# Two-layer second block of a fused kernel: the mixers' GpSimd work goes to VectorE and ScalarE, the rotation is done by small transfers, score products alternate between halves, one norm's squares are added on VectorE

## The chip, the cores and the metric

The kernel runs as one program on one core of one Trainium2 chip. The metric is the device time of an execution in microseconds. The kernel before has a median of 1934.74 us over three executions (1932.25 to 1937.94).

In the profile, PE is TensorE's matmul, PEld its weight load, DVE is VectorE, ACT is ScalarE, POOL is GpSimd and SP the engine that issues the weight loads.

## The reference, cut to what matters

Everything is fp32. A first block (a gated recurrence and a sparse attention, then a mixture of experts) turns x (256 tokens, 1024 wide) into a new x. A second block puts 16 learned tokens in front (272 tokens in all) and runs two layers, each a mixer and a gated feed-forward part. The change touches only the second block's layers:

```python
hn = rms_norm(h, norm_mix_g[l])
proj = hn @ w_in[l]
q, k, v, xr, gate = split(proj)                  # 512 columns each
q = apply_partial_rope(rms_norm(q, q_norm_g[l]), cos, sin)   # 4 heads x 2 halves x 64
k = apply_partial_rope(rms_norm(k, k_norm_g[l]), cos, sin)   # first 16 of 64 rotate
o_attn = diff_attention(q, k, v, lam)            # softmax(half 0) - lam * softmax(half 1)
o_rec = rg_lru_branch(xr, gate, ...)             # conv, two gates, a scan, gelu(gate)
h = h + concat(rms_norm(o_attn), rms_norm(o_rec)) @ w_out[l]
hn = rms_norm(h, norm_ffn_g[l])
g, u = split(hn @ w_gu[l])
h = h + (silu(g) * u) @ w_down[l]
```

The rotation takes, in each half of 64 channels, rows 0 to 7 and 8 to 15: x1 cos - x2 sin and x2 cos + x1 sin; the other 48 rows pass.

## The kernel before, in words

In the second block the activations are held with channels on partitions and tokens along the free side: `hT2` is 8 tiles of 128 channels by 272 tokens. A product `lin_f` (L323) makes 128 output channels: for each of 8 input tiles, three matmuls (the weight's high part by the input's high and low parts, the weight's low part by the input's high part), 24 in all, into one PSUM bank. Each weight piece, 128x1024, has to be split first: ScalarE rounds the high part (L1449), and VectorE (L1452) or, where the item says `eng`, GpSimd (L1454) subtracts for the low part. `run` (L294) issues the split of a piece LEAD = 4 products ahead of its use, and the split pieces have LEAD + 1 buffers. PSUM has 8 banks, taken in turn.

`layer2` (L1627) writes a layer as a list of items: four xr products with the convolution (`conv`), four k products (`qkin(4)` to `qkin(7)`) among which stand the recurrence's gates, four q products (`qkin(0)` to `qkin(3)`) among which stand the five steps of the recurrence's arithmetic (`lru1` to `lru5`, each on whole 128x1088 tiles), then four gate products (G), four value products (V), the attention's heads (`scores`, `mix`, `turn`, `value`), and the output product in two parts (R for the recurrence's half). The feed-forward part follows. A planner of the framework, which simulates the program, fixes the order of the instructions on each engine within this list; every engine then runs its own list in order. `high_priority` moves the small chains of a norm ahead.

The places that the change touches:

- `qkin(i)` (L1767): ScalarE takes the product out of PSUM as z (scaled) and as its square; VectorE writes product x cos into `qk`. `rope` (L1783), one product later, multiplies the squares by `comp` into the bank `prs` (L1787), multiplies z by the 128x128 matrix `rot` on TensorE (L1790), multiplies that by sin back into z (L1791) and adds z to `qk` (L1792). z lies in the tag "vin" with two buffers.
- `qk_norm` (L1794): once all eight squares are in `prs`, a chain of small VectorE instructions (L1800 to L1804, among them L209 to L213) makes the norm factors `rq`; `knorm` (L1807) spreads them by TensorE (`ps_rqb`, L1811) and multiplies `qk` by them.
- `lru2` to `lru4`, `gelu1`: four products of two 128x1088 tiles on GpSimd (L1711, L1717, L1718, L1724) and a fifth (L1740).
- G2, G3 and V0 to V3: the low parts of their weights on GpSimd (L1454).
- `rec_r` (L1757): the low part of the recurrence's output on GpSimd.
- `scores(h)` (L1837): for half 0 and then half 1 of a head, two or three products of 64 rows.
- `sum_h` (L1492): the sum of squares over channels for a norm, by TensorE with a column of ones; for each of the 8 tiles three products (two passes each), right after the tile is made. The norm "nm1", ahead of layer 1, has its sums among the down products of layer 0's feed-forward part.

The rest of GpSimd's work in the second block stays: in the feed-forward part, in the splits of the last output products and in the squares of the first norm.

Of the kernel before, what the change touches and what calls it, by code (L numbers as in the profile page):

```python
# [9 lines left out]
F32 = mybir.dt.float32  # L10
# [9 lines left out]
P = 128  # L20
T1 = 256
D = 1024
KT = 8
# [29 lines left out]

CONST = [("cos", T2), ("sin", T2), ("rot", 128)]
KO = {}
# [15 lines left out]
def _shape_constants():  # L71
    k = np.zeros((P, NCONST), np.float32)

    def put(name, a):
        o, w = KO[name]
        k[: a.shape[0], o : o + w] = a

    inv = np.float32(500000.0) ** (-np.arange(0, 16, 2, dtype=np.float32) / np.float32(16))
    ang = np.arange(T2, dtype=np.float32)[:, None] * inv[None, :]
    cos = np.ones((P, T2), np.float32)  # L80
    sin = np.zeros((P, T2), np.float32)
    rot = np.zeros((P, P), np.float32)
    for b in (0, 64):
        cos[b : b + 8] = np.cos(ang).T
        cos[b + 8 : b + 16] = np.cos(ang).T
        sin[b : b + 8] = np.sin(ang).T
        sin[b + 8 : b + 16] = np.sin(ang).T
        for i in range(8):
            rot[b + 8 + i, b + i] = -1.0
            rot[b + i, b + 8 + i] = 1.0  # L90
    put("cos", cos)
    put("sin", sin)
    put("rot", rot)
    return k
# [100 lines left out]
class Kernel:  # L195
# [1295 lines left out]
    def sum_h(self, pool, k, t0, name):  # L1491

        nc = self.nc
        n = T2 - t0
        ch = self.chunks(n)
        if k == 0:
            self.rb = None
            self.pss = self.ps(f"{name}ss")
        for j, (o, _) in enumerate(ch):
            nc.tensor.matmul(self.pss[:, j : j + 1], self.sq[k][:, o : o + P], self.ones[:, 0:1],  # L1500
                             start=(k == 0 and j == 0), stop=(k == KT - 1 and j == len(ch) - 1))
# [28 lines left out]
    def block2(self):  # L1530
        nc = self.nc
        self.rbs = [self.p2.tile([P, T2], F32, name=f"rb{i}", tag="rb") for i in range(4)]
        self.sq, self.pend, self.rb = {}, [], None
        items = []
        for l in range(2):
            items += self.layer2(l)
        yield from self.run(items, self.ph, LEAD, 8, True)
        hT = self.hT2
        for tt in range(2):
            for c in range(2):  # L1540
                ot = self.ph.tile([P, 1024], F32R, name=f"ot{tt}{c}", tag="whi").bitcast(F32)[:, 0:512]
                pt = self.ps(f"ps_out{tt}{c}")
                for k in range(4):
                    nc.tensor.transpose(pt[:, k * P : k * P + P],
                                        hT[:, 4 * c + k, NMETA + tt * P : NMETA + tt * P + P], self.ident)
                nc.scalar.copy(ot, pt)
                nc.sync.dma_start(self.out[tt * P : tt * P + P, c * 512 : c * 512 + 512], ot)

    def consts2(self, p2):
# [8 lines left out]

        self.cosT, self.sinT, self.rot = const("cos"), const("sin"), const("rot")

# [64 lines left out]
    def layer2(self, l):  # L1625
# [19 lines left out]
        def begin():  # L1645
# [59 lines left out]
        def lru2():  # L1705
            th, c, y, t = B["rr"], B["xc"], B["ry"], B["rt"]

            nc.vector.scalar_tensor_tensor(t, th, 1.0, c, op0=ALU.add, op1=ALU.mult)
            nc.vector.scalar_tensor_tensor(c, t, 2.0, c, op0=ALU.subtract, op1=ALU.mult)

            nc.gpsimd.tensor_tensor(t, y, y, op=ALU.mult)  # L1711

        def lru3():
            th, c, y, t, ii = B["rr"], B["xc"], B["ry"], B["rt"], B["ii"]
            nc.vector.scalar_tensor_tensor(t, t, -0.5, th, op0=ALU.mult, op1=ALU.mult)
            nc.vector.scalar_tensor_tensor(y, t, 1.5, y, op0=ALU.add, op1=ALU.mult)
            nc.gpsimd.tensor_tensor(ii, ii, c, op=ALU.mult)  # L1717
            nc.gpsimd.tensor_tensor(y, y, th, op=ALU.mult)  # L1718

        def lru4():  # L1720
            th, c, y, t, ii = B["rr"], B["xc"], B["ry"], B["rt"], B["ii"]

            nc.vector.tensor_scalar(y[:, :, 0:1], th[:, :, 0:1], 0.5, 0.5, op0=ALU.mult, op1=ALU.add)
            nc.gpsimd.tensor_tensor(ii, ii, y, op=ALU.mult)  # L1724
            nc.vector.tensor_scalar(t, c, -2.0, -1.0, op0=ALU.mult, op1=ALU.add)
# [32 lines left out]
        def rec_r():  # L1758
            hr = B["ry"]
            r = self.col_rows(B["recr"], T2, f"rec{l}")  # L1760
            for n in range(4):
                nc.vector.scalar_tensor_tensor(hr[:, n], hr[:, n], self.col("recg", 4 * l + n), r,
                                               op0=ALU.mult, op1=ALU.mult)
                self.split(part("yhi", 4 + n), part("ylo", 4 + n), hr[:, n], nc.gpsimd)


        def qkin(i):  # L1767
            def f(po):
# [8 lines left out]
                nc.scalar.activation(sq, po, AF.Square)  # L1777
                nc.vector.scalar_tensor_tensor(B["qk"][:, i], po, g, self.cosT, op0=ALU.mult, op1=ALU.mult)  # L1778
                if i != 4:
                    rope()  # L1780
                B["qs"] = i, sq, z
            return f

        def rope():
            i, sq, z = B["qs"]
# [50 lines left out]
        def scores(h):  # L1836
            def f():  # L1837
# [4 lines left out]
                mx = tile_(f"mx{h}", [P, 3, 2], tag="mx2", bufs=2)  # L1842
                pss = []
                for c in range(2):
                    s = slice(64 * c, 64 * c + 64)
                    ps = self.ps(f"ps_sc{l}{h}{c}")
                    nc.tensor.matmul(ps[:, 0:T2], qk[s, h, 144:272], qk[s, 4 + h, :], start=True, stop=True)
                    nc.tensor.matmul(ps[:, T2:416], qk[s, h, 16:144], qk[s, 4 + h, 0:144], start=True, stop=True)
                    if l == 0:
                        nc.tensor.matmul(ps[0:16, 416:432], qk[s, h, 0:16], qk[s, 4 + h, 0:16], start=True, stop=True)  # L1850
                    pss.append(ps)
                for c in range(2):
# [190 lines left out]
```

## Time and profile before

| | |
|---|---|
| median of three executions | 1934.74 us (1932.25 to 1937.94) |
| the profiled execution, its own time | 1937.82 us |
| its span, first to last instruction | 1936.1 us |
| busy over the span: PE / DVE / ACT / POOL | 1739.4 / 810.0 / 568.3 / 264.4 us |
| mean granted clock of TensorE | 0.935 of full |

The second block starts at about 1200 us and fills the rest of the span. Its layer 0 mixer lies at 1203 to 1362 us, layer 1's at 1590 to 1728 us. The time of an instruction is that between its start and its end, and instructions of one engine can overlap a little, so that start-to-start differences are the safer measure. The granted clock is 1.00 at 2.4 GHz and 0.50 at 1.2 GHz. A releaser in brackets is what ended the engine's idle time before the row.

### The profile page before, as it was taken

To read this page: it belongs to the slowest core of one execution; us is meant where nothing else is said; L and a number is where in the kernel's file an instruction comes from. 1 tells how busy PE (TensorE), PEld (TensorE's weight loads), DVE (VectorE), ACT (ScalarE), POOL (GpSimd) and SP (SyncE) were. 2 spreads that over 40 slices of the span, in tenths; PEclk is the share of its full clock that TensorE was granted. 3 is DMA by queue.
4 is the path that set the end of the run, shared out by engine and by line. 5 is a ranking of instruction groups with operands and counts; after the bars stand their busy time and mean duration, and the time that the engine had idled before them with its cause. 6 is when DMAs were issued, how large, how long until landed. Compare 5 with 4: busy or idle time off the path is not lost.

```text
span 1936.1 us, 34266 instructions
## 1 busy us (share of the span) xinstructions
PE 1739.4 (90%) x14551; PEld 1231.3 (64%) x14552; DVE 810.0 (42%) x1806; ACT 568.3 (29%) x1127; POOL 264.4 (14%) x259
## 2 busy tenths in 40 slices
PE   6999899866999997799999766989999998889998
PEld 3786743433544543454354334977999998789998
DVE  3573632211122222122222114587666557876653
ACT  2564511100111110011010102525544445354442
POOL 2322300000000000000000001051233103223320
PEclk8999889976999998899999878888999999889999
DMA  9658589999899999999999997220443453125441
GB/s 387 236 183 322 203 351 427 428 428 425 367 428 429 426 426 427 428 425 428 428 426 427 426 428 330 88 88 1 174 174 134 167 206 120 56 95 192 166 152 51
DMA packets 42698, 556.68 MB, mean 288 GB/s; under 512 B 4788, under 2 KB 5964, under 8 KB 8360
## 3 DMA queue, kind: packets, MB, share of 16 engines
q1 hardware_dynamic: 40368, 548.41, 69.4%
q0 software_dynamic: 1200, 4.29, 0.6%
q8 instruction: 116, 1.90, 0.4%
q10 hardware_dynamic: 968, 1.70, 0.3%
q14 instruction: 46, 0.38, 0.1%
HBM read 553.32 MB, written 1.06 MB: 286 GB/s over the span
## 4 chain that ended last, share of the span: by engine, by line
PE 56%; DMA 12%; DVE 5%; ACT 1%; issue 0%; ACTq 0%; POOL 0%; DVEq 0%; POOLq 0%
DMA we<-wexp 12%; PE ps_lin L339 9%; PE ps_lin L340 9%; PE ps_lin L341 9%; PE ps_l L1320 7%; PE ps_u L1320 6%; PE ps_d L1320 6%; PE ps_g L1286 2%; PE ps_c L1383 2%; DVE qk L1792 1%; PE ps_at L1363 1%; PE ps_rqb L1811 0%; PE ps_ri L1686 0%; PE ps_pg L1348 0%; PE nm0ss L1500 0%
## 5 line engine op out<-in xcount | busy, mean ns | idle before, releaser
L339 PE MATMUL ps_lin<-xhi,wh 128*128 128x272 f32 (+1 forms) x1024 | 301.6, 295 | 0.2 <-ACT xhi L1430 0.2
L340 PE MATMUL ps_lin<-xlo,wh 128*128 128x272 f32 (+1 forms) x1024 | 297.3, 291 | 1.0 <-DVE xlo L1431 1.0
L341 PE MATMUL ps_lin<-xhi,wl 128*128 128x272 f32 (+1 forms) x1024 | 297.4, 291 | 0.0
L1320 PE MATMUL ps_d<-we,at 128*32 128x256 f32 (+1 forms) x2048 | 223.0, 482 | 48.5 <-DMA we<-wexp 39.0
L1320 PE MATMUL ps_l<-we,xg 128*32 128x256 f32 (+1 forms) x2048 | 217.2, 461 | 29.7 <-DMA we<-wexp 29.5
L1320 PE MATMUL ps_u<-we,xg 128*32 128x256 f32 (+1 forms) x2048 | 212.4, 454 | 25.5 <-DMA we<-wexp 24.6
L339 PEld LDWEIGHTS ps_lin<-xhi,wh 128*128 128x128 f32 x1024 | 197.4, 193 | 2.8 <-DVE qk L1778 0.8
L340 PEld LDWEIGHTS ps_lin<-xlo,wh 128*128 128x128 f32 x1024 | 197.3, 193 | 1.8 <-DVE xlo L1431 1.4
L341 PEld LDWEIGHTS ps_lin<-xhi,wl 128*128 128x128 f32 x1024 | 197.3, 193 | 0.0
L1320 PEld LDWEIGHTS ps_d<-we,at 128*32 128x32 f32 (+1 forms) x2048 | 90.4, 128 | 165.0 <-issue 102.2
L1320 PEld LDWEIGHTS ps_l<-we,xg 128*32 128x32 f32 (+1 forms) x2048 | 88.6, 123 | 139.4 <-issue 97.2
L1320 PEld LDWEIGHTS ps_u<-we,xg 128*32 128x32 f32 (+1 forms) x2048 | 87.1, 121 | 128.0 <-issue 76.1
L1387 DVE TENSOR_TENSOR hT<-hT,ps_c 128x512 f32<-128x512 f32 x128 | 79.4, 681 | 151.7 <-PE ps_c L1383 151.7
L1406 POOL TENSOR_TENSOR hT<-hT,g 128x1024 f32<-128x1024 f32 x1 | 3.3, 3261 | 946.1 <-DVE ssm L1404 946.1
L1449 ACT CAST wh<-wgu 128x1024 fp32r<-128x1024 f32 x88 | 92.2, 1049 | 122.1 <-PE ps_lin L340 121.4
L1452 DVE TENSOR_TENSOR wl<-wgu,wh 128x1024 fp32r<-128x1024 f32 x88 | 108.2, 1231 | 41.6 <-ACT wh L1449 41.6
L1332 DVE TENSOR_SCALAR gl<-ps_u 128x512 f32<-128x512 f32 (+1 forms) x36 | 20.3, 572 | 217.1 <-PE ps_u L1324 217.1
L1364 ACT COPY at<-ps_at 128x512 f32<-128x512 f32 (+1 forms) x36 | 17.3, 492 | 299.9 <-PE ps_at L1363 299.1
L339 PE MATMUL ps_lin<-ahi,wh 128*128 128x272 f32 (+1 forms) x352 | 100.6, 286 | 0.0
L341 PE MATMUL ps_lin<-ahi,wl 128*128 128x272 f32 (+1 forms) x352 | 100.0, 284 | 0.0
L340 PE MATMUL ps_lin<-alo,wh 128*128 128x272 f32 (+1 forms) x352 | 99.9, 284 | 0.0
L1288 ACT ACTIVATE xg<-ps_g,modc,a2c 128x128 f32<-128x128 f32 (+1 forms) x120 | 43.8, 452 | 171.0 <-PE ps_g L1286 171.0
(677 smaller groups left out, 2920.9 us busy)
## 6 DMA issues: line engine op xcount, KB each, us to landing
we<-wexp SPq DMA_DIRECT2D x192, 2048.0 KB, 27.3
wgu<-wgu SPq DMA_DIRECT2D x22, 2048.0 KB, 7.7
win<-win SPq DMA_DIRECT2D x14, 2048.0 KB, 9.1
wada<-wada SPq DMA_DIRECT2D x12, 2048.0 KB, 7.9
wdn<-wdn SPq DMA_DIRECT2D x16, 1408.0 KB, 6.0
wout<-wout SPq DMA_DIRECT2D x6, 2048.0 KB, 7.7
wint<-wint SPq DMA_DIRECT2D x2, 2048.0 KB, 9.3
wins<-wins SPq DMA_DIRECT2D x1, 1264.0 KB, 28.1
```

Source lines behind the costliest of these rows:

```text
L339: nc.tensor.matmul(po[:m, :nn], hi[:, a], xh[k], start=(k == 0), stop=False)
L340: nc.tensor.matmul(po[:m, :nn], hi[:, a], xl[k], start=False, stop=False)
L341: nc.tensor.matmul(po[:m, :nn], lo[:, a], xh[k], start=False, stop=(k == nk - 1))
L1286: nc.tensor.matmul(p, self.x[:, tt, k * P : k * P + P], oh[:, tt], start=(tt == 0), stop=(tt == 1))
L1288: nc.scalar.activation(xg[:, k], pg[:, (k - k0) * n : (k - k0) * n + n], AF.Identity, scale=self.a2c[:, k : k + 1], bias=self.modc2[:, k : ...
L1320: nc.tensor.matmul(dst[b][s], lhs(k, b), ws[k // 4][:, o : o + wd], start=(k == 0 and b % per == 0), stop=False)
L1332: nc.vector.tensor_scalar(gl[i], pu[i], 7.0, 0.5, op0=ALU.min, op1=ALU.mult)
L1363: nc.tensor.transpose(pt[:, c * P : c * P + P], li[i][:, c * P : c * P + P], self.ident)
L1383: nc.tensor.matmul(pc[s][:, (tt - t0) * wd : (tt - t0) * wd + wd], gt[b][rows[s], tt * P : tt * P + P], y[b // per][rows[s], (b % per) * w ...
L1387: nc.vector.tensor_tensor(a, a, pc[s].rearrange("p (a b) -> p a b", a=per), op=ALU.add)
L1449: nc.scalar.copy(hi, src)
L1452: nc.vector.tensor_tensor(lo, src, hi.bitcast(F32), op=ALU.subtract)
```

## The change

The rotation's matrix product goes. Instead `qkin` issues, on ScalarE's queue, four transfers of 8 partitions by 272 tokens each, which copy rows of z to the other place in a tile `zr` (two of these for the layer, cleared once by GpSimd); the sign moves into the sin table. `rope` multiplies `zr` by sin into a new tile `zs` (tag "vin", the one of z) and adds that to `qk`. The five 128x1088 products of GpSimd go to VectorE, except the square in `lru2`, which goes to ScalarE. The weights' low parts of G2, G3 and V0 to V3 and the low part in `rec_r` go to VectorE. `scores` writes the products of half 0 and half 1 in turn. For "nm1" VectorE adds the squares of tiles 0 to 6 into one tile `nsum`, and TensorE sums only `nsum` and tile 7.

```diff
@@ sum_h
+        few = name == "nm1"
...
+        if few and 0 < k < KT - 1:
+            nc.vector.tensor_tensor(self.nsum[:, :n], (sq[0] if k == 1 else self.nsum)[:, :n], sq[k][:, :n], op=ALU.add)
+        if k == (KT - 1 if few else 0):
             self.pss = self.ps(f"{name}ss")
...
+        for i, a in enumerate(([self.nsum, sq[k]] if k == KT - 1 else []) if few else [sq[k]]):
+            for j, (o, _) in enumerate(ch):
+                nc.tensor.matmul(self.pss[:, j : j + 1], a[:, o : o + P], self.ones[:, 0:1],
...
@@ begin
+            for n in range(2):
+                B["zr", n] = tile_(f"zr{n}", [P, T2])
+                nc.gpsimd.memset(B["zr", n], 0.0)
@@ lru2, lru3, lru4, gelu1
-            nc.gpsimd.tensor_tensor(t, y, y, op=ALU.mult)
+            nc.scalar.activation(t, y, AF.Square)
-            nc.gpsimd.tensor_tensor(ii, ii, c, op=ALU.mult)
-            nc.gpsimd.tensor_tensor(y, y, th, op=ALU.mult)
+            nc.vector.tensor_tensor(ii, ii, c, op=ALU.mult)
+            nc.vector.tensor_tensor(y, y, th, op=ALU.mult)
-            nc.gpsimd.tensor_tensor(ii, ii, y, op=ALU.mult)
+            nc.vector.tensor_tensor(ii, ii, y, op=ALU.mult)
-            nc.gpsimd.tensor_tensor(t, t, gl, op=ALU.mult)
+            nc.vector.tensor_tensor(t, t, gl, op=ALU.mult)
@@ rec_r
-                self.split(part("yhi", 4 + n), part("ylo", 4 + n), hr[:, n], nc.gpsimd)
+                self.split(part("yhi", 4 + n), part("ylo", 4 + n), hr[:, n], nc.vector)
@@ qkin
+                zr = B["zr", i % 2]
+                for o in (0, 8):
+                    for h in (0, 64):
+                        nc.scalar.dma_start(zr[h + 8 - o : h + 16 - o], z[h + o : h + o + 8])
                 if i != 4:
                     rope()
-                B["qs"] = i, sq, z
+                B["qs"] = i, sq, zr
@@ rope
-            prt = self.ps(f"ps_rot{l}{i}")
-            nc.tensor.matmul(prt[:, :T2], self.rot, z, start=True, stop=True)
-            nc.vector.tensor_tensor(z, prt[:, :T2], self.sinT, op=ALU.mult)
-            nc.vector.tensor_tensor(B["qk"][:, i], B["qk"][:, i], z, op=ALU.add)
+            t = tile_(f"zs{i}", [P, T2], tag="vin", bufs=2)
+            nc.vector.tensor_tensor(t, zr, self.sinT, op=ALU.mult)
+            nc.vector.tensor_tensor(B["qk"][:, i], B["qk"][:, i], t, op=ALU.add)
@@ scores
-                    nc.tensor.matmul(ps[:, 0:T2], qk[s, h, 144:272], qk[s, 4 + h, :], start=True, stop=True)
-                    nc.tensor.matmul(ps[:, T2:416], qk[s, h, 16:144], qk[s, 4 + h, 0:144], start=True, stop=True)
...
+                for rows, o, q, w in parts:
+                    for c in range(2):
+                        s = slice(64 * c, 64 * c + 64)
+                        nc.tensor.matmul(pss[c][rows, o : o + w], qk[s, h, q : q + rows.stop], qk[s, 4 + h, 0:w], start=True, stop=True)
@@ the lists
-        G = [inp(1, n, gate(n), pool if n > 1 else None) for n in range(4)]
-        V = [inp(4, n, vin(n), pool) for n in range(4)]
+        G = [inp(1, n, gate(n)) for n in range(4)]
+        V = [inp(4, n, vin(n)) for n in range(4)]
```

## Rows read from the trace of the kernel before

**Rows 1.** Stretches: from:to, length, busy time of engines, TensorE clock, DMA share

```profile
1247.00:1259.00 12.00, 10.72 (x80) 10.04 (x79) 7.32 (x11) 11.72 (x15) 1.39 (x1) 1.00 0.22 93
1254.00:1287.00 33.00, 22.87 (x151) 21.73 (x150) 31.89 (x36) 10.34 (x16) 25.14 (x9) 0.85 0.18 65
1287.00:1296.00 9.00, 9.00 (x55) 7.85 (x53) 3.37 (x7) 1.04 (x1) 0.00 (x0) 0.59 0.00 0
1296.00:1328.00 32.00, 32.00 (x237) 27.44 (x237) 28.19 (x140) 20.64 (x66) 4.87 (x2) 1.00 0.19 67
1500.00:1590.00 90.00, 90.00 (x727) 90.00 (x726) 44.98 (x57) 36.84 (x53) 8.15 (x7) 1.00 0.53 193
```

**Rows 2.** PE's waits from 1240 us on: waiter, releaser, total, times, longest

```profile
PE ps_rqb L1811 <- DVE rq_y L1804: 11.5, 2, 6.1
PE ps_rot L1790 <- ACT z L1775: 10.7, 6, 4.1
PE ps_lin L340 <- POOL ylo L1454: 0.8, 2, 0.5
```

**Rows 3.** PE in order of time: start, length, instruction, idle time before it

```profile
1234.88 0.70 PE L1790 MATMUL ps_rot<-z,rot 128*128 128x272 f32 x2
1235.51 2.05 PE L1686 MATMUL ps_ri<-xc,wrec 64*64 64x272 f32 x16
...
1286.73 2.83 PE L1811 MATMUL ps_rqb<-ident,rq_y 128*64 128x128 f32 x24 [5.42 <-DVE rq_y L1804]
...
1294.88 0.72 PE L1847 MATMUL ps_sc<-qk 64*128 64x272 f32 x2
...
1296.95 0.88 PE L1811 MATMUL ps_rqb<-ident,rq_y 128*64 128x128 f32 x12
...
1557.37 0.72 PE L1500 MATMUL nm1ss<-ones,nm1sq 128*128 128x1 f32 x6
1557.96 0.38 PE L339 MATMUL ps_lin<-ahi,wh 128*128 128x272 f32 x1
...
1664.46 0.74 PE L1847 MATMUL ps_sc<-qk 64*128 64x272 f32 x4
```

**Rows 4.** VectorE's groups, 1210 us to the end: count, busy us, mean ns, idle before

```profile
L1452 DVE TENSOR_TENSOR wl<-win,wh 128x1024 fp32r<-128x1024 f32 x23 | 28.2, 1224 | 21.9 <-ACT wh L1449 21.9
L1792 DVE TENSOR_TENSOR qk<-qk,z 128x272 f32<-128x272 f32 x16 | 19.5, 1219 | 0.2
L1715 DVE SCALAR_TENSOR_TENSOR rt<-rt,rr 128x1088 f32<-128x1088 f32 x2 | 7.2, 3602 | 0.0
L1716 DVE SCALAR_TENSOR_TENSOR ry<-rt,ry 128x1088 f32<-128x1088 f32 x2 | 6.7, 3358 | 0.1
L1725 DVE TENSOR_SCALAR rt<-xc 128x1088 f32<-128x1088 f32 x2 | 5.1, 2556 | 0.0
L1802 DVE TENSOR_SCALAR rqv<-rqv 128x48 f32<-128x48 f32 x2 | 4.3, 2126 | 0.1
L1709 DVE SCALAR_TENSOR_TENSOR xc<-rt,xc 128x1088 f32<-128x1088 f32 x2 | 2.6, 1282 | 0.0
```

**Rows 5.** VectorE in order of time, the addition of a rotation beside an idle GpSimd

```profile
1255.84 0.43 DVE L1792 TENSOR_TENSOR qk<-qk,z 128x272 f32<-128x272 f32 x1
```

**Rows 6.** GpSimd's and ScalarE's groups, same stretch and columns as Rows 4

```profile
L1454 POOL TENSOR_TENSOR wl<-win,wh 128x1024 fp32r<-128x1024 f32 x12 | 33.3, 2785 | 23.4 <-ACT wh L1449 12.0 <-PE ps_sc L1850 11.3
L1449 ACT CAST wh<-win 128x1024 fp32r<-128x1024 f32 x34 | 35.6, 1046 | 86.6 <-PE ps_lin L340 86.6
```

**Rows 7.** ScalarE in order of time, the last q product of layer 0

```profile
1273.24 0.49 ACT L1775 ACTIVATE z<-ps_lin,qgs 128x272 f32<-128x272 f32 x1 [6.75 <-DVE qk L1792]
```

**Rows 8.** Issues on ScalarE's queue: count, ns each (shortest, median, longest), starts

```profile
L824 ACTq DMA_DIRECT2D bt<-bexp x2: 334/346/359, 203.0 to 203.5; - x2
```

**Rows 9.** Transfers by line: queue, count, KB each, median us from issue to landing

```profile
out<-ot SPq DMA_DIRECT2D x4, 256.0 KB, 2.1
bt<-bexp ACTq DMA_DIRECT2D x2, 192.0 KB, 5.5
```

More of the change, by code (lines that the diff above doesn't have):

```diff
@@ L52 @@
 NCOL = _o
-CONST = [("cos", T2), ("sin", T2), ("rot", 128)]
+CONST = [("cos", T2), ("sin", T2)]
 KO = {}
@@ L81, in _shape_constants @@
     sin = np.zeros((P, T2), np.float32)
-    rot = np.zeros((P, P), np.float32)
     for b in (0, 64):
@@ L85, in _shape_constants @@
         cos[b + 8 : b + 16] = np.cos(ang).T
-        sin[b : b + 8] = np.sin(ang).T
+        sin[b : b + 8] = -np.sin(ang).T
         sin[b + 8 : b + 16] = np.sin(ang).T
-        for i in range(8):
-            rot[b + 8 + i, b + i] = -1.0
-            rot[b + i, b + 8 + i] = 1.0
     put("cos", cos)
     put("sin", sin)
-    put("rot", rot)
     return k
@@ L1495, in sum_h @@
         ch = self.chunks(n)
+        sq = self.sq
+        few = name == "nm1"
         if k == 0:
             self.rb = None
+        if few and 0 < k < KT - 1:
+            nc.vector.tensor_tensor(self.nsum[:, :n], (sq[0] if k == 1 else self.nsum)[:, :n], sq[k][:, :n], op=ALU.add)
+        if k == (KT - 1 if few else 0):
             self.pss = self.ps(f"{name}ss")
-        for j, (o, _) in enumerate(ch):
-            nc.tensor.matmul(self.pss[:, j : j + 1], self.sq[k][:, o : o + P], self.ones[:, 0:1],
-                             start=(k == 0 and j == 0), stop=(k == KT - 1 and j == len(ch) - 1))
+        for i, a in enumerate(([self.nsum, sq[k]] if k == KT - 1 else []) if few else [sq[k]]):
+            for j, (o, _) in enumerate(ch):
+                nc.tensor.matmul(self.pss[:, j : j + 1], a[:, o : o + P], self.ones[:, 0:1],
+                                 start=(i == 0 and j == 0 and (few or k == 0)), stop=(k == KT - 1 and a is sq[k] and j == len(ch) - 1))
         if k == KT - 1:
@@ L1532, in block2 @@
         self.rbs = [self.p2.tile([P, T2], F32, name=f"rb{i}", tag="rb") for i in range(4)]
+        self.nsum = self.p2.tile([P, T2], F32, name="nsum")
         self.sq, self.pend, self.rb = {}, [], None
@@ L1557, in const @@
             return t
-        self.cosT, self.sinT, self.rot = const("cos"), const("sin"), const("rot")
+        self.cosT, self.sinT = const("cos"), const("sin")
         self.m2 = m2 = p2.tile([P, 416], F32, name="m2")
@@ L1778, in f @@
                 nc.vector.scalar_tensor_tensor(B["qk"][:, i], po, g, self.cosT, op0=ALU.mult, op1=ALU.mult)
+                zr = B["zr", i % 2]
+                for o in (0, 8):
+                    for h in (0, 64):
+                        nc.scalar.dma_start(zr[h + 8 - o : h + 16 - o], z[h + o : h + o + 8])
                 if i != 4:
                     rope()
-                B["qs"] = i, sq, z
+                B["qs"] = i, sq, zr
             return f
         def rope():
-            i, sq, z = B["qs"]
+            i, sq, zr = B["qs"]
             for j, (o, _) in enumerate(self.chunks(T2)):
@@ L1842, in f @@
                 mx = tile_(f"mx{h}", [P, 3, 2], tag="mx2", bufs=2)
[L1843 to L1846, printed above, removed]
-                    nc.tensor.matmul(ps[:, 0:T2], qk[s, h, 144:272], qk[s, 4 + h, :], start=True, stop=True)
-                    nc.tensor.matmul(ps[:, T2:416], qk[s, h, 16:144], qk[s, 4 + h, 0:144], start=True, stop=True)
-                    if l == 0:
-                        nc.tensor.matmul(ps[0:16, 416:432], qk[s, h, 0:16], qk[s, 4 + h, 0:16], start=True, stop=True)
-                    pss.append(ps)
+                pss = [self.ps(f"ps_sc{l}{h}{c}") for c in range(2)]
+                parts = [(slice(0, P), 0, 144, T2), (slice(0, P), T2, 16, 144)] + ([(slice(0, 16), 416, 0, 16)] if l == 0 else [])
+                for rows, o, q, w in parts:
+                    for c in range(2):
+                        s = slice(64 * c, 64 * c + 64)
+                        nc.tensor.matmul(pss[c][rows, o : o + w], qk[s, h, q : q + rows.stop], qk[s, 4 + h, 0:w], start=True, stop=True)
                 for c in range(2):
```

## The prediction

> **What bounds the kernel now.** I read the page's shares first: TensorE is busy over most of the span, so a change in the second block pays only where TensorE waits, runs at the lower clock, or does work that goes. Then the stretches: in layer 0's feed-forward part TensorE is busy for 90.00 of 90 us at full clock, while from 1254 to 1287 us, where the q products and the recurrence's arithmetic lie, it is busy for 22.87 of 33 us, and VectorE for 31.89 with GpSimd beside it for 25.14 [rows 1]. So that stretch is VectorE's, the feed-forward part TensorE's. Then TensorE's waits: the two largest are the norm factors (11.5 us over the two layers) and z for the rotation (10.7 us) [rows 2]. They are one thing: z of the last q product waits 6.75 us for a buffer that VectorE's addition L1792 holds [rows 7], and the chain for the norm factors stands behind the same VectorE work. TensorE goes on at 1286.73 us [rows 3] and then runs at a mean clock of 0.59 for 9 us [rows 1].
>
> Last, VectorE's groups, for why it is late. The addition L1792 takes 0.43 us with GpSimd idle [rows 5] but 1.219 us in the mean of 16; L1715, L1716 and L1725 take 3.60, 3.36 and 2.56 us where L1709, of the same width and with GpSimd idle, takes 1.28; L1802 takes 2.13 us for 48 columns, less work than the 0.43 us addition of 272 [rows 4, 5]. VectorE stands still beside GpSimd's long instructions. Over both layers this loses 16 x (1.219 - 0.43) = 12.6, 7.2 + 6.7 + 5.1 - 6 x 1.28 = 11.3, and four such halts in the norm-factor chain (two in a layer; L1802's row stands for them) of 2.13 less at most 0.43, some 6.8: in all 30.7 us, 15.4 a layer, nearly all in the 33 us stretch.
>
> **The change part by part**, against the profiled execution's 1937.82 us (span 1936.1 and 1.7 around it), which is 3.1 above the median.
>
> *GpSimd out of the mixers.* VectorE gets back 15.4 us a layer and takes over, before the norm factors, three products of 1088 columns at 1.28 us [rows 4] and five weight pieces at 1.22 us (23 of that shape are there already [rows 4]; GpSimd needs 2.79 us each [rows 6]): 3.8 + 6.1 = 9.9 us. If VectorE stays full up to the norm factors, they come 15.4 - 9.9 = 5.5 us earlier in each layer: the lower end. The upper end is ScalarE. It is busy 11.72 of the 12 us up to 1259 [rows 1]; three projections' transfers at four issues of 0.35 us [rows 8] add 4.2 us and the Square of 1088 columns about 1.05, as the 1024-wide cast [rows 6]: 1264.2 us. Then come two more projections, each a cast of 1.05, a z of 0.49 and a square taken as long [rows 6, 7], with one set of issues (1.4) between: the last square ends at 1269.7 instead of about 1274.2 (1273.24 + 2 x 0.49 [rows 7]), 4.5 us earlier. Behind it the old path took 1286.73 - 1274.2 = 12.5 us, with two halts of the chain (3.4) and the last two additions' halts (about 1.6 together by the mean) in it: 5.0 go. Upper end 9.5 us. I take 7.5: VectorE's full row [rows 1] speaks for the lower end, but the chain is moved ahead of other ready work and needs neither the recurrence's products nor V's weights, which can fall behind it. That is 15 us over two layers. Work that falls behind is paid later: VectorE has 32 - 28.19 us of room up to 1328 us [rows 1].
>
> *The rotation.* One rotation on TensorE costs 0.63 us from start to start (1234.88 to 1235.51) [rows 3]. The two that stand ahead of all the gates delay the recurrence's arithmetic: 1.3 us a layer, 2.5 in all; the other two k rotations, ahead of the table loads and q, move the stretch by up to as much again, and I take 1.5 of it. Rotations of q lie in VectorE's stretch and give nothing. The wait of z on L1792 goes (it is in the term above). What is late next is the transfers: L1792 now waits for four landings. The nearest small transfer lands 2.1 us after its issue, one on ScalarE's queue beside the weight loads 5.5 us [rows 9]. `rope` runs a product later (24 matmuls), which covers the first; behind VectorE's wait stand the next product's x cos and the weight pieces, so a late landing stops TensorE after some products. From 0 to 2.1 us for each of the 8 q projections, 0 to 17; I take 3, since VectorE is behind anyway and the DMA share there is 0.18 [rows 1]. On ScalarE each projection's issues (1.4 us) delay what stands behind them: the next weight cast, which leads by four products, the next z and the gates. For the k products the room is there (the gates lie between), for q it is in the sum above.
>
> The Trainium skill ("DMA: Bandwidth & Descriptors", section "Rules for kernel authors") speaks against this part: transfers under 64 KB are mostly overhead, and many small ones should be joined into a large one. The 64 pieces here are of 8.5 KB. The rows agree that an issue costs the same 0.33 to 0.36 us whatever its size is for [rows 8]; the trace has no transfer this small. By the rule, read as four overheads in series of 2.1 us per projection, the third rival below is what comes.
>
> *Halves in turn.* In layer 0 a head's products take 1296.95 - 1294.88 = 2.07 us, half after half. In layer 1 the planner's order already has both halves' long products side by side: four instructions in 0.74 us where two take 0.72 [rows 3]. So layer 0 gains half of 2.07, 1.03 for each of 4 heads, 4.1 us, and layer 1 nothing. TensorE is full there (32.00 of 32), but VectorE is at 28.19 and gets L1740's product and one more weight piece (2.5 us) for a halt it loses: I take 3, with 0 and 4.1 as ends.
>
> *The norm's squares.* Each of the 8 sums takes 1557.96 - 1557.37 = 0.59 us [rows 3] in the stretch where TensorE is always busy; six go: 3.5 us in full. The six additions are 0.43 us each [rows 5] on a VectorE that is busy 44.98 of 90 us [rows 1]; if that cover failed, 2.6.
>
> *The rest.* `rec_r`'s low part costs TensorE 0.8 us of waits [rows 2]; I take 0.5. The clearing of `zr` lies at a layer's begin beside products; bounds 0 to 1. SP's weight loads wait for pieces to be split, and none of TensorE's larger waits is for them: nothing.
>
> Sum: 15 + 4 - 3 + 3 + 3.5 + 0.5 = 23 us. 1937.8 - 23 = 1914.8 on the profiled execution, which stands 3.1 above the median; so **1912** for the median.
>
> **The rivals.**
>
> *VectorE stays the bound, or waits for landings.* The norm factors come 5.5 us earlier at best, eight landings take some 1.5 each back (12), the scores gain nothing: 11 - 12 + 2.5 + 3.5 = 5 to 10 us, 1925 to 1930. For it: 31.89 of 33. Against it: the DMA share there is low.
>
> *TensorE stops stalling.* With the planner's order now near the truth, the chain comes right behind the last square: 9.5 us a layer, no low clock behind the stall (9 us at 0.59 instead of 1.00, 3.7 us a layer [rows 1]), the full rotation and score terms: 2 x (9.5 + 3.7) + 5 + 4.1 + 3.5 + 0.8 = 40, and 1895. For it: the two waits are 22.2 us [rows 2]. Against it: 9.9 us more work on VectorE.
>
> *The transfers become the pace: slower.* z is freed only by its four landings, and `zs` uses the same two buffers. If that puts cast, z, square, issues and landing in a row, a q projection takes 1.05 + 0.98 + 1.4 + L. The stretch's 151 matmul records in 33 us [rows 1] are about six products of 24, one in 5.5 us, stalls included. With L = 2.1 it is 5.5: the stretch gains nothing. With 5.5, as beside the weight loads, it is 8.9: 3.4 us for each of 8 projections, 27 in all, less 7 of the last three terms: slower by 20, 1955. It decides from L of about 3 on. By the Trainium skill's rule in series (4 x 2.1) it is worse still. Against it: there are two buffers, and the DMA share is 0.18 [rows 1].
>
> *No change.* Gains in the mixers are paid back before the output product, since VectorE's total grows where it had 3.8 us of room; only the 3.5 of the norm and a little stay: 1930 to 1936.
>
> **How the numbers follow.** Forecast (14 to 32 us gained) 0.47; TensorE stops stalling 0.16; VectorE or landings bound 0.18; no change 0.10; slower 0.09. A difference under 0.3% (5.8 us) can't be told from none here. Faster: 0.47 + 0.16 and nearly all of 0.18, so 0.80; same: 0.11; slower: 0.09. The range from 1890 to 1931 holds the first three cases and leaves out most of the last two and the far end of the second.
>
> **What would show it.** Right: L1715, L1716 at about 1.3 us and L1792 at 0.43; TensorE's wait on the norm factors under 4 us a layer; nothing waiting as ps_rot; layer 0's heads at about 1.05 us of score products; 12 instead of 48 nm1ss matmuls. Wrong: TensorE's wait at L1811 as long as before (VectorE bound); VectorE's L1791 or L1792 with idle time released by a DMA of more than 1 us each, or ScalarE's z waiting for landings (third rival); a second half (1296 to 1362) that grew by what the first lost (no change).

## The result: 1915.15 us, and the profile after

The kernel after takes 1915.15 us (median of 4 runs, 1911.26 to 1917.45) against 1934.95 (4 runs): ratio 0.9899, interval 0.9886 to 0.9912. That is 19.8 us less; forecast were 1912 and 22.7. The profiled execution took 1911.26 us, its span 1909.5.

The halts are gone. VectorE's groups (line, operation, tiles, count, busy us, mean ns, idle before) against [rows 4]. The lines have moved: L1715, L1716 and L1725 of the kernel before are L1722, L1723 and L1732 of this one, L1792 is L1802 and L1802 is L1812. The first two take 1.28 us where they took 3.60 and 3.36, the third 0.72 (2.56 before), the additions 0.435 in the mean of 16 (1.219), and the 48 columns 0.18 (2.13).

```profile
L1722 DVE SCALAR_TENSOR_TENSOR rt<-rt,rr 128x1088 f32<-128x1088 f32 x2 | 2.6, 1282 | 0.0
L1723 DVE SCALAR_TENSOR_TENSOR ry<-rt,ry 128x1088 f32<-128x1088 f32 x2 | 2.6, 1281 | 0.0
L1732 DVE TENSOR_SCALAR rt<-xc 128x1088 f32<-128x1088 f32 x2 | 1.4, 716 | 0.0
L1812 DVE TENSOR_SCALAR rqv<-rqv 128x48 f32<-128x48 f32 x2 | 0.4, 184 | 0.0
L1801 DVE TENSOR_TENSOR zs<-zr,sin 128x272 f32<-128x272 f32 x16 | 7.0, 438 | 13.7 <-DMA zr<-z 13.6
L1802 DVE TENSOR_TENSOR qk<-qk,zs 128x272 f32<-128x272 f32 x16 | 6.9, 435 | 0.2
```

But TensorE's wait on the norm factors, 11.5 us in [rows 2], has doubled. From the lists of waits (total, times, longest): TensorE's for the rotation are gone, waits on the squares `qsq` have come, those on the recurrence's low part `ylo` are 1.7 us where they were 0.8 [rows 2], and VectorE waits for the landed rows of `zr`:

```profile
PE ps_rqb L1821 <- DVE rq_y L1814: 22.8, 2, 12.4
PE ps_qs L1798 <- ACT qsq L1784: 6.6, 2, 3.5
PE ps_lin L335 <- DVE ylo L1449: 1.7, 2, 0.9
DVE zs L1801 <- DMA zr<-z: 13.6, 9, 3.3
```

Layer 0 on TensorE (start, us, idle before): the last squares' sums are 3.13 us late, the factors 12.43, and a head's scores take 1.12 us where they took 2.07 [rows 3].

```profile
1264.36 0.84 PE L1798 MATMUL ps_qs<-comp,qsq 128*128 128x16 f32 x6 [3.13 <-ACT qsq L1784]
1277.63 2.83 PE L1821 MATMUL ps_rqb<-ident,rq_y 128*64 128x128 f32 x24 [12.43 <-DVE rq_y L1814]
1284.80 1.12 PE L1859 MATMUL ps_sc<-qk 64*128 64x272 f32 x12
```

VectorE between those two moments: the 13 links of the factors' chain take 0.2 us each, yet it lasts from 1266.42 to 1277.58, because a recurrence product, landings, scans and two weight pieces stand between the links.

```profile
1266.42 0.19 DVE L1810 SCALAR_TENSOR_TENSOR rqv<-ps_qs,r 128x48 f32<-128x48 f32 x1
...
1266.75 1.28 DVE L1731 TENSOR_TENSOR ii<-ii,ry 128x1088 f32<-128x1088 f32 x1
1267.95 0.18 DVE L204 TENSOR_SCALAR rq_y<-rqv 128x48 int32<-128x48 int32 x1
1268.54 0.44 DVE L1801 TENSOR_TENSOR zs<-zr,sin 128x272 f32<-128x272 f32 x1 [0.40 <-DMA zr<-z]
1269.64 0.44 DVE L1801 TENSOR_TENSOR zs<-zr,sin 128x272 f32<-128x272 f32 x1 [0.67 <-DMA zr<-z]
1270.01 1.33 DVE L1736 TENSOR_TENSOR_SCAN ry<-rt,ii 128x272 f32<-128x272 f32 x2
1271.25 0.18 DVE L206 TENSOR_TENSOR rq_t<-rq_y 128x48 f32<-128x48 f32 x1
1271.35 1.33 DVE L1736 TENSOR_TENSOR_SCAN ry<-rt,ii 128x272 f32<-128x272 f32 x2
1272.60 0.77 DVE L1802 TENSOR_TENSOR qk<-qk,zs 128x272 f32<-128x272 f32 x2
...
1275.11 2.35 DVE L1447 TENSOR_TENSOR wl<-win,wh 128x1024 fp32r<-128x1024 f32 x2
1277.38 0.20 DVE L1814 TENSOR_TENSOR rq_y<-rq_y,nm0r_y 128x48 f32<-128x48 f32 x1
```

ScalarE and its queue (ACTq): an issue takes 0.63 us in the median of 64 (least, median and most in ns in the first line), instead of the 0.35 of [rows 8]. In layer 0 the last three issues of a projection take 2.18 us together, and ScalarE's next instruction (ACT_TABLE_LOAD) stands behind them.

```profile
L1789 ACTq DMA_DIRECT2D zr<-z x64: 631/632/1232, 1226.8 to 1626.7; - x64
1242.14 2.18 ACTq L1789 DMA_DIRECT2D zr<-z  x3
1244.36 1.28 ACT L1707 ACT_TABLE_LOAD   x1 [2.12 <-issue]
```

The trace before has one transfer on that queue that is smaller than those of [rows 8], 24 KB at the kernel's start:

```profile
L284 ACTq DMA_DIRECT2D bada<-bada x1: 775/775/775, 1.3 to 1.3; - x1
```

Stretches of the kernel after (busy us of TensorE, weight loads, VectorE, ScalarE, GpSimd; granted clock): q products to factors, factors to scores, and scores. VectorE is busy 24.81 of 28 us in the first, where it was 31.89 of 33 [rows 1]: it now waits, while the clock is 0.79 and then 0.72 of full speed.

```profile
1250.00:1278.00 28.00, 12.44 (x103) 12.24 (x103) 24.81 (x45) 10.82 (x15) 0.00 (x0) 0.79 0.23 80
1278.00:1287.00 9.00, 9.00 (x74) 7.67 (x71) 2.46 (x4) 1.04 (x1) 0.00 (x0) 0.72 0.01 3
1287.00:1319.00 32.00, 27.87 (x214) 24.09 (x213) 27.42 (x140) 20.68 (x65) 0.00 (x0) 0.95 0.19 67
```

The norm's sums are now 12 matmuls (line, instructions, ns):

```profile
L1502 PE MATMUL nm1ss<-ones,nsum x6: 167/250/250, 1570.4 to 1570.9; 128*128 128x1 f32 x6
L1502 PE MATMUL nm1ss<-ones,nm1sq x6: 165/250/250, 1572.1 to 1572.6; 128*128 128x1 f32 x6
```

### The profile page after: what moved, and what is told of

It reads as the page before. It is cut to its first block, busy times and chain, and to the rows that moved or that the text cites. A ratio compares the mean times of both kernels' runs of the same rounds, so it can differ in the third digit from the quotient of the medians.

```text
span 1909.5 us, 34235 instructions
## 1 busy us (share of the span) xinstructions
PE 1698.6 (89%) x14483; PEld 1204.0 (63%) x14484; DVE 798.8 (42%) x1840; ACT 569.4 (30%) x1129; POOL 198.8 (10%) x232
## 5 line engine op out<-in xcount | busy, mean ns | idle before, releaser
L334 PE MATMUL ps_lin<-xhi,wh 128*128 128x272 f32 (+1 forms) x1024 | 297.1, 291 | 0.0
L1315 PE MATMUL ps_d<-we,at 128*32 128x256 f32 (+1 forms) x2048 | 219.6, 475 | 45.9 <-DMA we<-wexp 35.2
L1315 PE MATMUL ps_l<-we,xg 128*32 128x256 f32 (+1 forms) x2048 | 213.2, 452 | 30.0 <-DMA we<-wexp 29.2
L1283 ACT ACTIVATE xg<-ps_g,modc,a2c 128x128 f32<-128x128 f32 (+1 forms) x120 | 43.9, 453 | 170.2 <-PE ps_g L1281 170.2
```

What stands on the lines that cost most here:

```text
L334: nc.tensor.matmul(po[:m, :nn], hi[:, a], xh[k], start=(k == 0), stop=False)
L1283: nc.scalar.activation(xg[:, k], pg[:, (k - k0) * n : (k - k0) * n + n], AF.Identity, scale=self.a2c[:, k : k + 1], bias=self.modc2[:, k : ...
L1315: nc.tensor.matmul(dst[b][s], lhs(k, b), ws[k // 4][:, o : o + wd], start=(k == 0 and b % per == 0), stop=False)
```

## The experiments

Theory: GpSimd's leaving is the gain, and the rest of the change adds little because VectorE and ScalarE, not TensorE, are late at the norm factors. Rivals: the transfers or the alternation carry it; VectorE only moves its work. Ratios are to the kernel before, with 95% intervals; "block" is the second block's length in the profiled execution, from its first product to the output's transposes. Both measures are needed: the work ahead of the second block, whose steps no run changes, takes between 1192.5 us (u_rot) and 1203.3 us (dma_hold) in these traces, so that a time alone does not tell kernels a few us apart.

| kernel | median us | ratio, interval | block us |
|---|---|---|---|
| before | 1934.0 to 1935.0 | 1 | 732.0 |
| after | 1915.15 | 0.9899 [0.9886, 0.9912] | 708.6 |
| u_rot: rotation undone | 1912.80 | 0.9891 [0.9877, 0.9905] | 709.8 |
| u_pool: GpSimd back | 1931.82 | 0.9986 [0.9977, 0.9995] | 724.8 |
| u_sc: alternation undone | 1912.71 | 0.9886 [0.9871, 0.9900] | 708.8 |
| u_nm1: norm's sums undone | 1915.90 | 0.9902 [0.9887, 0.9916] | 711.8 |
| a_pool: GpSimd's leaving alone | 1911.76 | 0.9878 [0.9863, 0.9893] | 716.1 |
| a_pool2: the same again | 1914.75 | 0.9898 [0.9881, 0.9914] | 708.1 |
| rot_sc: GpSimd's leaving, norm's sums | 1909.96 | 0.9876 [0.9859, 0.9892] | 704.4 |
| dma_pool: issued by GpSimd | 1912.05 | 0.9883 [0.9868, 0.9899] | 704.0 |
| hold: recurrence held | 1905.48 | 0.9841 [0.9828, 0.9855] | 701.4 |
| rot_hold | 1906.59 | 0.9849 [0.9835, 0.9862] | 699.0 |
| dma_hold | 1906.57 | 0.9859 [0.9842, 0.9875] | 693.9 |
| rot_sc_hold | 1913.81 | 0.9898 [0.9882, 0.9915] | 708.8 |

Three stages of those traces, each from the start of one TensorE group to the start of the next, layer 0 / layer 1:

| stage (us) | before | after | u_rot | u_pool | a_pool | a_pool2 | dma_pool | hold | rot_hold |
|---|---|---|---|---|---|---|---|---|---|
| gates to norm factors | 51.2 / 51.2 | 48.8 / 47.8 | 45.9 / 45.8 | 52.5 / 51.6 | 45.8 / 45.8 | 45.9 / 45.8 | 45.6 / 45.6 | 43.5 / 44.5 | 40.4 / 40.4 |
| scores to output products | 41.3 / 37.1 | 41.0 / 33.8 | 41.0 / 33.8 | 39.4 / 38.8 | 39.1 / 33.8 | 39.1 / 33.8 | 41.1 / 33.8 | 37.6 / 34.5 | 43.2 / 35.2 |
| from there to `ro*3r` | 19.2 / 18.0 | 17.1 / 15.4 | 20.2 / 15.4 | 21.3 / 19.0 | 19.8 / 18.5 | 15.6 / 17.0 | 17.1 / 17.0 | 20.2 / 17.0 | 18.7 / 14.4 |

**u_rot.** The rotation goes back to TensorE, everything else stays as after.

```diff
...
-                        nc.scalar.dma_start(zr[h + 8 - o : h + 16 - o], z[h + o : h + o + 8])
...
+            nc.tensor.matmul(prt[:, :T2], self.rot, z, start=True, stop=True)
-            nc.vector.tensor_tensor(t, zr, self.sinT, op=ALU.mult)
+            nc.vector.tensor_tensor(z, prt[:, :T2], self.sinT, op=ALU.mult)
...
```

> The changed kernel with the rotation on TensorE again (matrix rot, z rewritten in place, no transfers, no zr). Changed kernel: 1915. Theory: the four issues of a projection take 0.63 us each of ScalarE, 20 us a layer, and hold up the last square, so the transfers give back what the rotation's matmuls cost; without them 1909 to 1917, TensorE's wait for qsq (6.6 us) gone, its wait for the norm factors still 15 us or more, because VectorE's fillers stay. Rival (the rotation by transfers is the larger part of the 20 us gain): 1924 to 1931.

1912.8: the theory's time; the wait on the factors is 7.4 us a layer, 14.8 and just under its "15 or more". The transfers gain nothing; in the stage up to the norm factors they cost 2.9 and 2.0 us. The blocks are as long all the same because two other stretches of layer 0 are shorter with transfers: the first products up to the gates by 3.4 us and the stage behind the first output product by 3.1. In both the clock differs too (0.86 and 0.72 up to `nm0r`, 0.90 and 0.75 behind the output product), so that how much of it is the planner's order no run shows.

**u_pool and a_pool.** GpSimd comes back, or leaves alone (the kernel before with only these lines changed).

```diff
...
-            nc.vector.tensor_tensor(ii, ii, c, op=ALU.mult)
-            nc.vector.tensor_tensor(y, y, th, op=ALU.mult)
+            nc.gpsimd.tensor_tensor(ii, ii, c, op=ALU.mult)
+            nc.gpsimd.tensor_tensor(y, y, th, op=ALU.mult)
...
-        V = [inp(4, n, vin(n)) for n in range(4)]
+        V = [inp(4, n, vin(n), pool) for n in range(4)]
```

> The changed kernel with GpSimd in the mixers again (the five wide products, the low parts of G2, G3, V0 to V3 and of rec_r), the rest as changed. Theory (VectorE's halts beside GpSimd are what the change removes): 1925 to 1934, with L1792's counterpart back at over 1 us and the wide VectorE products at over 3. Rival (moving the work to VectorE only swaps halts for work): 1912 to 1918.

> The kernel before with one of the four parts alone: the second block's mixers without GpSimd (products, sums and splits go to VectorE, the first square of the recurrence to ScalarE). Rotation on TensorE, halves' scores in order and the norm's squares summed tile by tile, as before. Theory (GpSimd's leaving is the gain, and the norm's squares add 3.9 us on their own, as the stage table of the kernel with that part undone shows: 202.4 against 198.5 us): the kernel with the rotation undone was 1912.8, so with 3.9 more 1916.7, forecast 1915 to 1919; the wait of TensorE on the norm factors stays at 6 to 8 us a layer. Rival (the gain needs VectorE to be relieved of the rotation's waits or of scores at once): 1922 to 1930.

The theory's time held for u_pool (1931.82). The additions are back at 1.04 us, the wide instructions L1722, L1723 and L1732 at 2.36, 2.20 and 2.58, not over 3. a_pool went past its theory: 1911.76, all of the gain. Its stretch from the gates to the factors in layer 0 and the same stretch of the kernel before, both with 281 matmuls (columns as above): with GpSimd's 25.14 us gone VectorE is busy 5.3 us less, although it has more to do, and the stretch is 5.4 us shorter. The wait on the factors is 7.4 us a layer. The last line is the recurrence's scans in a_pool's stretch, which came behind the factors before.

```profile
1232.40:1278.20 45.80, 37.15 (x281) 33.64 (x280) 35.81 (x62) 26.13 (x41) 0.00 (x0) 0.96 0.26 93
```

```profile
1235.50:1286.70 51.20, 40.44 (x281) 36.67 (x280) 41.08 (x51) 24.94 (x40) 25.14 (x9) 0.91 0.23 83
```

```profile
L1737 DVE TENSOR_TENSOR_SCAN ry<-rt,ii 128x272 f32<-128x272 f32 x4 | 2.6, 700 | 0.0
```

**a_pool2.** The block of a_pool's trace was 716.1 us long, too long for its median, so the same kernel ran again.

> The kernel with GpSimd's leaving as its only part once more, because its two readings disagree: by the median (1911.76) it has the whole gain, by the second block's length in the trace (716.1 us from its first product to the transposes of the output, 732.0 before, 708.6 after) two thirds. Theory (the length is right, and three of its four runs were fast for a reason that is not the part's: they show a granted clock of 0.949 where the profiled one shows 0.945): most runs 1914 to 1919. Rival (the part alone does give all): most runs 1910 to 1913 again, and this trace's second block is some 708 us long.

It split the two: runs of 1910.81, 1914.7, 1914.8 and 1915.2, and a block of 708.1. The largest difference between the two traces is the clock in one stage. The same 91 matmuls in layer 0's stage behind the first output product (TensorE busy, granted clock), in a_pool and in a_pool2:

```profile
1324.80:1344.70 19.90, 17.03 (x91) 0.74 0.00 1
```

```profile
1327.80:1343.40 15.60, 12.75 (x91) 1.00 0.00 1
```

So the part alone gives 19 to 23 us, and a single trace is good to some 8 us of block length, while its stage up to the norm factors repeats to 0.1.

The same can be read for the whole block. TensorE from the second block's first product to the output's transposes (length, busy us, granted clock) in the kernel before, a_pool, a_pool2 and the kernel after:

```profile
1196.60:1928.60 732.00, 696.90 (x5331) 0.95 0.34 125
1193.40:1909.50 716.10, 688.84 (x5331) 0.96 0.35 128
1197.30:1905.40 708.10, 680.86 (x5331) 0.97 0.35 129
1193.30:1901.90 708.60, 664.74 (x5263) 0.96 0.36 130
```

With GpSimd's leaving alone TensorE's idle time falls from 35.1 to 27.2 or 27.3 us, in both runs alike. The rest, 8.1 us in a_pool and 16.0 in a_pool2, is the same 5331 matmuls taking less time at a higher clock. Up to the norm factors it is VectorE's chain that ends the stage, so those 10.7 us over two layers, alike in both runs, are VectorE's. The other 5.2 us of a_pool and 13.2 of a_pool2 lie in other stages and differ by the clock; what of them GpSimd's leaving causes no run separates. In the kernel after TensorE idles for 43.9 us, more than before; what is saved there is busy time.

**u_sc, u_nm1 and rot_sc.** The halves' scores go back to one half after the other, the norm's squares to 48 matmuls (`few = False`), or rotation and scores both go back.

```diff
-                for rows, o, q, w in parts:
-                    for c in range(2):
+                for c in range(2):
+                    s = slice(64 * c, 64 * c + 64)
+                    nc.tensor.matmul(ps[:, 0:T2], qk[s, h, 144:272], qk[s, 4 + h, :], start=True, stop=True)
...
-        few = name == "nm1"
+        few = False
```

> The changed kernel with the score products half after half again. Theory (in layer 0's head section VectorE is the pace, so TensorE's 4 us there go into waits): 1915 to 1917. Rival (the 4.1 us are saved in full): 1918.5 to 1920.

> The changed kernel with nm1's squares summed by TensorE tile by tile again (48 products). Theory (TensorE is the pace of the feed-forward part): 3.5 us more, 1918 to 1920. Rival (planner's order or waits hide it): 1914 to 1916.

> The kernel after with rotation and scores as before the change: GpSimd out of the mixers and the norm's squares added by VectorE are what is left. Theory (parts add up: 716.1 us for the first alone less 3.9 for the second): length 710 to 713, time 1910 to 1914. Rival (transfers or alternation carry a part of the gain when taken away together): length above 715, time 1916 to 1922.

u_sc came out below both expectations: alternation gives nothing here, and layer 0's stage from scores to output products is 39.1 us without it, 41.0 with it. TensorE in that stage, in the kernel after and in u_sc:

```profile
1284.80:1325.80 41.00, 35.83 (x278) 0.96 0.15 52
```

```profile
1286.90:1326.00 39.10, 38.07 (x277) 1.00 0.15 55
```

With alternation TensorE is idle for 5.2 us, without it for 1.0, and its clock is 0.96 with the waits and 1.00 without. u_nm1's median (1915.9) fits the rival and can't be told from after's, but the stage from `nf0r` to `nm1r` is 202.4 us in it and 198.5 in after. rot_sc, without transfers and alternation, is at 1909.96 no slower than after; its median lies at the lower end of its theory, its block (704.4) below it.

**dma_pool.** The 64 small transfers are issued by GpSimd.

```diff
-                        nc.scalar.dma_start(zr[h + 8 - o : h + 16 - o], z[h + o : h + o + 8])
+                        nc.gpsimd.dma_start(zr[h + 8 - o : h + 16 - o], z[h + o : h + o + 8])
```

> The kernel after with the 64 small transfers of the rotation issued by GpSimd, which has nothing else to do in the mixers, and not by ScalarE. Theory (the issues of 0.63 us each hold ScalarE, and the squares that TensorE waits for come late by it): ScalarE's stalls go, TensorE's waits on the squares (6.6 us between 1180 and 1910) fall under 3, time 1910 to 1913.5, as with the rotation on TensorE. Rival (the landing is the price, or issuing by GpSimd costs more than by ScalarE and halts or delays VectorE): 1915 to 1922, with VectorE's waits for the landed rows above the 13.6 us of the kernel after.

1912.05, within the theory's time, though its interval overlaps that of the kernel after. An issue takes 0.50 us on GpSimd (ns: least, median, most), and VectorE's waits on landings fall from 13.6 to 4.9 us (the last two lines are who waited for the landings, total and times):

```profile
L1789 POOL DMA_DIRECT2D zr<-z x64: 497/499/638, 1230.9 to 1628.5; - x64
...
  ACT z L1782: 7.1, 2
  DVE zs L1801: 4.9, 2
```

The stage up to the factors is 45.6 us in both layers, as short as with the rotation on TensorE: what the transfers cost there goes with their issues when ScalarE is rid of them. The landing is not free: ScalarE's z now waits 7.1 us for it, since its buffer is held until the rows have landed, and TensorE's waits on the squares grew instead of falling (4.8 and 4.6 us in the two layers against 3.1 and 3.5).

**hold.** The recurrence's second half (`lru3` to `lru5`) is held until the factors are done, by a constant that is read from a column written behind them.

```diff
+                nc.vector.tensor_scalar(B["mh"], B["rq"][:, 1, 0:1], 0.0, -0.5, op0=ALU.mult, op1=ALU.add)
...
-            nc.vector.scalar_tensor_tensor(t, t, -0.5, th, op0=ALU.mult, op1=ALU.mult)
+            nc.vector.scalar_tensor_tensor(t, t, B["mh"], th, op0=ALU.mult, op1=ALU.mult)
...
-               inp(3, 3, qkin(7)), lru1, inp(2, 0, qkin(0)), lru2, inp(2, 1, qkin(1)), lru3, inp(2, 2, qkin(2)), lru4,
-               inp(2, 3, qkin(3)), lru5]
+               inp(3, 3, qkin(7)), lru1, inp(2, 0, qkin(0)), lru2, inp(2, 1, qkin(1)), inp(2, 2, qkin(2)), inp(2, 3, qkin(3))]
...
-        it += [G[0], qk_norm, G[1], knorm(4), knorm(5), G[2], scores(0), knorm(6), G[3], scores(1),
+        it += [G[0], qk_norm, G[1], knorm(4), knorm(5), lru3, G[2], scores(0), lru4, lru5, knorm(6), G[3], scores(1),
```

> The kernel after with the second half of the recurrence (the last step of its square root, its products and scans) held until the norm factors are done: its first instruction takes its constant from a column that one small added instruction writes behind the factors. Theory (the factors' chain of 13 links of 0.2 us takes 11 us because the planner puts the recurrence's wide products of 1.3 us, its scans and splits between the links): TensorE's wait on the factors falls from about 11 us a layer to 3 to 6, and the time to 1900 to 1909. Rival (VectorE has the same work to do before the end of the mixer and is late somewhere else instead): the wait falls, the stages behind it grow by as much, 1912 to 1918.

1905.48, with an interval apart from after's: the fillers were a part of the wait, and VectorE has room for them later. The wait fell from 12.4 and 10.3 us to 8.4 and 8.0, not under 6. VectorE in layer 0: eleven links in 2.6 us, then two landings and two weight pieces still stand among the last.

```profile
1270.37 0.21 DVE L1810 SCALAR_TENSOR_TENSOR rqv<-ps_qs,r 128x48 f32<-128x48 f32 x1 [0.47 <-PE ps_qs L1798]
...
1272.76 0.21 DVE L207 SCALAR_TENSOR_TENSOR rq_t<-rq_t,rqv 128x48 f32<-128x48 f32 x1
1274.52 0.44 DVE L1801 TENSOR_TENSOR zs<-zr,sin 128x272 f32<-128x272 f32 x1 [1.56 <-DMA zr<-z]
1274.88 0.20 DVE L208 SCALAR_TENSOR_TENSOR rq_y<-rq_t,rq_y 128x48 f32<-128x48 f32 x1
1275.42 0.44 DVE L1801 TENSOR_TENSOR zs<-zr,sin 128x272 f32<-128x272 f32 x1 [0.34 <-DMA zr<-z]
1275.78 2.35 DVE L1447 TENSOR_TENSOR wl<-win,wh 128x1024 fp32r<-128x1024 f32 x2
...
1278.40 0.20 DVE L1814 TENSOR_TENSOR rq_y<-rq_y,nm0r_y 128x48 f32<-128x48 f32 x1
```

**rot_hold, dma_hold, rot_sc_hold.** Hold together with u_rot, with dma_pool, and with rot_sc.

> As the kernel with the recurrence held until the norm factors are done, but with the rotation on TensorE as before the change. Theory (without transfers nothing else fills the chain, so the wait is shortest here): the wait on the factors 2 to 4 us a layer, time 1897 to 1907, up to 4 us under the kernel with transfers and held recurrence. Rival (VectorE pays later): 1910 to 1915, as with the rotation undone alone (1912.8).

> Two edits at once on the kernel after: transfers of the rotation issued by GpSimd, and the recurrence's second half held until the norm factors are done. Theory (the two remove different halves of the wait: ScalarE's issue time, 4.6 us of block length alone, and the fillers in the chain, 7.2 us alone): length 697 to 700 us, time 1900 to 1904, TensorE's wait on the factors under 4 us a layer. Rival (both remove the same wait): length 701 to 704, time 1905 to 1909.

> The kernel after with the rotation on TensorE and the halves' scores in order, both as before the change, and the recurrence's second half held until the norm factors are done. Theory (of the change only GpSimd's leaving and the norm's sums pay, and the transfers and the alternation can go without loss): 1903 to 1907, as with the rotation undone and the recurrence held (1906.6, length 699.0). Rival (alternation pays once the wait in front of the scores is short, by up to 4 us as reckoned before the change): 1908 to 1911, length 702 to 704.

rot_hold has its theory's time (1906.59), and the wait on the factors is 2.1 us in each layer; but scores to output products is 2.2 us longer in layer 0 than with the rotation undone alone: VectorE has the recurrence's second half to do there, and TensorE waits 5.1 us for `e` instead of 2.7. dma_hold has the shortest block of all, 693.9 us, shorter even than its theory, a wait on the factors of 5.4 us a layer, not under 4, and a median (1906.57) like the two others, which is its rival's. In its trace the work ahead of the second block takes longest of all (1203.3 us), so the two measures disagree: not settled. All three with the recurrence held and the alternation kept beat both kernels, the one after by some 9 us and the one before by 28; which is best these runs don't tell.

rot_sc_hold missed: 1913.81, slower than even its rival expected. It differs from rot_hold in the order of the halves alone, so with the wait on the factors short the alternation pays. TensorE in rot_hold, from scores to output products of layer 0, the same of layer 1, and the stage behind that (busy us, granted clock):

```profile
1283.70:1326.80 43.10, 36.95 (x277) 0.92 0.14 50
1638.80:1674.00 35.20, 32.09 (x251) 1.00 0.17 61
1674.00:1688.40 14.40, 10.93 (x82) 0.98 0.00 1
```

and in rot_sc_hold:

```profile
1281.20:1328.10 46.90, 42.59 (x278) 0.89 0.13 46
1641.50:1676.80 35.30, 32.17 (x252) 1.00 0.16 61
1676.80:1695.60 18.80, 15.39 (x82) 0.73 0.00 0
```

In layer 0 the stage is 3.8 us shorter with alternation. That it is near the 4.1 of the prediction is partly chance: the prediction reckoned with a full TensorE, and here it is idle for 6.2 us in rot_hold and 4.3 in rot_sc_hold, at a clock of 0.92 and 0.89. In layer 1 the products cost the same, and the 4.4 us behind them are the clock: the same 82 matmuls at 0.98 and at 0.73. At least 4.4 of the 9.8 us between the two blocks are thus the clock's, and why it is lower without alternation no run shows.

## Why the prediction was right, and which terms were not

The time came within 3.2 us of the forecast, by the mechanism that was named first; but errors of the terms cancelled, and that is luck.

- **GpSimd out of the mixers: 15 forecast, 19 to 23 measured (a_pool, a_pool2).** The halts were where the prediction put them. Up to the norm factors the gain was the lower end (5.5 forecast, 5.4 measured in each layer, 10.7 together), so VectorE's full row was the right sign and the 7.5 taken was too much. That 5.4 is so near to 5.5 is luck in part. By VectorE's groups in layer 0's stretch the halts were 16.7 us, not 15.4 (from the kernel before to a_pool the additions fall from 9.8 us to 3.5, L1715, L1716 and L1725 from 9.6 to 3.3, the chain's L213 and L1802 from 4.9 to 0.8); L1725 was measured against an instruction with two inputs and alone takes 0.72 us, not 1.28. Against that stand, besides the 9.9 us that were reckoned, the scans, 2.6 us, which now come ahead of the factors. What the prediction left out lies behind the factors: in a_pool2 the stages from the scores to `ro*3r` are 10.1 us shorter over both layers (2.2 and 3.3, then 3.6 and 1.0), where it expected work to be paid back. Some 7 of these 10 us are the clock (the same matmuls keep TensorE busy for 104.0 us before and 97.0 in a_pool2) and some 3 are waits.
- **The rotation: +4 - 3 forecast, about -2 measured (1915.15 against 1912.80, within what the runs can tell).** The landing was the wrong price. The issue was taken at 0.35 us, from transfers of 192 KB [rows 8, 9], as if it did not depend on the transfer. [rows 8] can't show that, since both of its issues are of one size, and the trace before has a counterexample on the same queue, a transfer of 24 KB at the kernel's start whose issue took 0.775 us. In the kernel after an issue measures 0.63, so a projection holds ScalarE for 2.5 us, not 1.4; moved to GpSimd, the cost in that stage is gone. The Trainium skill ("DMA: Bandwidth & Descriptors", section "Rules for kernel authors") calls such small transfers mostly overhead. The trace agrees in that these pay by the piece: 64 x 0.63 = 40 us of ScalarE for 0.5 MB. Read as four landings in a row, as the third rival did, it would have cost far more than the 2.9 and 2.0 us of u_rot's comparison. One sign of that rival did come, VectorE's waits for landed rows (13.6 us in 9 waits), but without its price.
- **The halves in turn: 3 forecast, nothing measured.** The step held (1.12 us a head, 1.05 forecast). What failed is the cover: TensorE was full there (32.00 of 32 us [rows 1]) and is busy 27.87 of 32 after, waiting for VectorE, so that shorter products only lengthen its wait (5.2 us idle in that stage against 1.0 in u_sc). Where the wait on the factors is short the stage is 3.8 us shorter with alternation (rot_hold, rot_sc_hold), a part of it through the clock.
- **The norm's squares: 3.5 forecast, 3.9 measured** in their stage.
- **`rec_r`: 0.5 forecast, a loss of 0.9 measured.** TensorE waits 1.7 us for `ylo` over both layers, split by VectorE, where it waited 0.8 for GpSimd.
- **"TensorE's wait on the norm factors under 4 us a layer": wrong, 12.4 and 10.3.** The text took the chain to run "ahead of other ready work". It does not in VectorE's list above: other ready work stands between the links, and a 1.3 us product in a gap delays the link behind it. By its own list this sign said "VectorE bound"; what was late were fillers in the chain, and the squares of ScalarE. With the fillers held and no transfers the wait is 2.1 us, and the time some 9 us lower: a part of the rival "TensorE stops stalling" was to be had, by another order.

Still open: why an issue takes 0.63 us here; whether transfers issued by GpSimd beat the rotation on TensorE, once the recurrence is held; which of GpSimd's jobs, the wide products or the low parts, carries the gain, since every run moves them together; and what of the higher clock belongs to the change.

## What to carry to other kernels

When a stage that was hardly touched gets shorter, compare its busy time and its granted clock before putting it down to the change: here some 7 of the 10 us behind the factors were the same matmuls at a higher clock. Take the price of an issue from a transfer of the same shape, or call it unknown. A short chain of dependent instructions with high priority is still slow when its planner may put long ready work between the links: hold that work behind the chain by data. And undo each part of a change alone: here one of four gave nearly all, and two gave nothing that could be measured.

## What the runs showed of the hardware

- Beside GpSimd's arithmetic a VectorE addition of 272 columns took 1.219 us in the mean and 0.435 without it, an instruction on 48 columns 2.13 and 0.18.
- Issuing a transfer of 8 partitions by 272 numbers takes 0.63 us on ScalarE's queue and 0.50 on GpSimd, and the ScalarE instruction behind three of them started when they were done, after 2.12 us. VectorE's additions keep their 0.435 us beside GpSimd's issues (dma_pool).
- Two traces of the same code differ by 8 us of block length, 4.3 of it in one stage through the granted clock alone (91 matmuls in 15.6 us at 1.00, in 19.9 at 0.74). A stage's length is compared together with its clock.
